# One-hot products in 32 bits, the weight's two parts side by side, four tokens at a time, multiplied on GpSimd

## The chip, the core and the metric

The kernel runs on one core of a Trainium2 chip. The core has TensorE (PE in the rows; PEld is its weight load), VectorE (DVE), ScalarE (ACT), GpSimd (POOL) and SyncE (SP, which issues most of the DMAs). The metric is the device time of one launch in microseconds (us). Before the change it is 2845.25 us, the median of three runs (2843.61 to 2845.64).

## The reference

One transformer layer for 256 prompt tokens and 64 sample tokens of 2048 features: differential attention, a gated chunk MLP, attention to a memory, a gated sum, an output projection, and then a PEER layer, a mixture of 16384 single-row experts. The last layer is where the change is:

```python
def _peer_block(xb, w_query, sub_keys, expert_u, expert_v):
    q = (xb @ w_query).reshape(tb, PEER_HEADS, 2, PEER_HALF)
    s = jnp.einsum('thpc,hpkc->thpk', q, sub_keys).astype(jnp.float32)
    s1, i1 = lax.top_k(s[:, :, 0], PEER_TOPK)
    s2, i2 = lax.top_k(s[:, :, 1], PEER_TOPK)
    ...
    eidx = jnp.take_along_axis(cand_i, top_j, axis=-1)
    g = jax.nn.softmax(top_s, axis=-1).astype(xb.dtype)
    a = jax.nn.gelu(jnp.einsum('td,thkd->thk', xb, expert_u[eidx]), approximate=False)
    return jnp.einsum('thk,thkd->td', g * a, expert_v[eidx])
```

Each token has 8 heads times 16 chosen experts, 128 pairs of an expert and a weight g. An expert's number is 128 * i0 + i1, with i0 and i1 from 0 to 127.

## The kernel before, in words

All instructions are recorded by one Python program that keeps a clock for each engine from assumed costs (the class `Plan`, and `pe_cost`, `dve_cost`, `pool_cost`). Work is cut into tasks (generators); a task goes on when the plan's TensorE clock has passed the assumed end of what it waits for. So the costs and these due times set in which order each engine gets its instructions, and each engine then runs its own list strictly in that order.

TensorE works through a stream of weight pieces. Each half of a piece is loaded by SP into a ring `raw`, ScalarE copies it to `hi` (a 32-bit form with a shorter mantissa, fp32r), VectorE makes `lo` = raw - hi, and TensorE multiplies with hi and lo (class `Stream`, line 413). A ring of four halves of hi and lo lies between VectorE and TensorE. In the PEER layer two phases follow each other. In the first, 128 pieces called Up (16 blocks of three 128x256 products each) compute gelu(x . u) for 256 of the tokens and all 16384 experts; the result goes to `hs`, and for 28 of 32 groups to DRAM. In the second, 128 pieces called Down multiply the weighted hs with expert_v.

The other 64 tokens don't use these dense products. For them GpSimd gathers rows of expert_u and then expert_v (128 indirect DMAs of 1 MB each, tiles `r` and `gs`, queues POOL), and VectorE makes a dot product or a weighted sum from each one (2048 elements a partition: `dots` and `x2s`). These gathers run through both phases.

The dense path needs, for each token t, the 128 x 128 table G_t[i0, i1] of weights, zero where no expert was chosen. It is built by TensorE as a product of one-hot matrices: over the token's 128 choices, one-hot(i0) transposed times (one-hot(i1) * g). That is the task `g_unit` (line 1447), 32 times for 8 tokens each, started by `weights_lane` (line 1339) when Up piece 36 + 74 * t0 / 256 is done, so spread over Up pieces 36 to 110. A unit before the change: VectorE compares `io` (0 to 127) with i0 and i1 (tile `oa`, two operations), multiplies the second with the three bf16 parts of g (tile `ob`, three operations; all 128x1024 in bf16), TensorE makes 3 products of 128x128 for each token (lines 1461 and, through `mm`, 271), added up in PSUM banks `bk`, ScalarE copies each bank of four tokens to `st`, and each 16 tokens SP writes `st` to DRAM (`gd`). When all of them are there, the tables are read back for the Down phase (`gg`).

The task `decode` (line 1365) makes the columns i0, i1 and the parts of g with the token along the free dimension. Line 271 in a row is the helper that records every instruction of VectorE, ScalarE and GpSimd and some of TensorE; tiles tell them apart.

## Time and profile before

| | before |
|---|---|
| median of three runs | 2845.25 us |
| the profiled execution | 2845.33 us, of which the span from first to last instruction 2843.6 us |
| busy: PE, DVE, ACT, POOL | 2788.7, 1870.9, 1101.7, 472.7 us |
| mean granted TensorE clock | 0.963 of 2.4 GHz |
| moved by DMA | 634.75 MB, 223 GB/s over the span |

A group row reads: line, engine, operation, output tile <- input tiles, shapes, count, then busy time in us (overlaps counted once), mean duration in ns, and idle time of the engine just before these instructions with what ended it. Matmuls are pipelined: a duration of 300 ns is longer than the distance to the next start, so rates are read from starts or from counts over a stretch.

### The profile page before, as it was taken

The numbers are of one execution on the slowest core, as the hardware profiler recorded it, in microseconds if no ns is written. First come the engines' busy times: TensorE is split into PE (matmuls) and PEld (weight loads), VectorE is DVE, ScalarE is ACT, GpSimd is POOL, SyncE is SP. The second block draws the span as 40 slices with busy tenths as digits, with TensorE's granted clock in tenths as the row PEclk, the third lists the DMA queues.
The fourth block names the chain that finished last, engine by engine and source line by source line (L and its number), as shares of the span: only waits on it lengthen the run. The fifth ranks groups of instructions, "written<-read, shape, count | busy, mean of one in ns | idle before, by whom it ended". The sixth has DMA issues, their size and how long they took to land.

```text
span 2843.6 us, 42779 instructions
## 1 busy us (share of the span) xinstructions
PE 2788.7 (98%) x17350; PEld 2556.7 (90%) x17350; DVE 1870.9 (66%) x2673; ACT 1101.7 (39%) x1449; POOL 472.7 (17%) x459
## 2 busy tenths in 40 slices
PE   7899999999999999999999999999999899999999
PEld 5899899999999999999899989898997787888887
DVE  8446665444445578898655655555678887888884
ACT  4343444333333343454333333333443334344443
POOL 6423431000001231111100010000112120211100
PEclk9899999999999999999888988888999999999999
DMA  7534343444444544668676666676889888899984
GB/s 220 157 116 126 120 129 124 149 149 151 151 151 156 172 153 163 199 224 283 245 260 234 244 246 230 238 243 229 319 296 330 319 321 294 326 366 341 329 288 140
DMA packets 231909, 634.75 MB, mean 223 GB/s; under 512 B 15776, under 2 KB 70048, under 8 KB 213152
## 3 DMA queue, kind: packets, MB, share of 16 engines
q1 hardware_dynamic: 206624, 474.58, 49.9%
q0 software_dynamic: 21056, 142.76, 13.4%
q10 hardware_dynamic: 4032, 14.68, 1.3%
q8 instruction: 136, 2.23, 0.3%
q14 instruction: 61, 0.50, 0.0%
HBM read 594.08 MB, written 37.88 MB: 222 GB/s over the span
## 4 chain that ended last, share of the span: by engine, by line
PE 85%; DVE 3%; DMA 2%; ACT 1%; issue 1%; ACTq 0%; DVEq 0%
PE mm L413 75%; PE bk L271 5%; PE bk L1461 4%; DMA raw<-pv 2%; DVE lo L271 1%; ACT hi L271 1%; DVE x2s L271 1%; DVE xb L271 0%; ACT xb L271 0%; DVE hs L271 0%; DVE x2t L271 0%; DVE e L271 0%; DVE w L271 0%; ACT w L271 0%; DVE vt L271 0%
## 5 line engine op out<-in xcount | busy, mean ns | idle before, releaser
L271 DVE TENSOR_TENSOR lo<-raw,hi 128x1024 fp32r<-128x1024 f32 (+1 forms) x622 | 874.2, 1408 | 815.2 <-ACT hi L271 814.7
L271 ACT ACTIVATE hi<-raw 128x1024 fp32r<-128x1024 f32 (+1 forms) x622 | 731.5, 1177 | 1052.8 <-PE mm L413 841.4
L413 PE MATMUL mm<-xb,hi 128*128 128x256 f32 x4096 | 802.9, 298 | 0.0
L413 PEld LDWEIGHTS mm<-xb,hi 128*128 128x128 f32 x4096 | 686.1, 205 | 6.3
L413 PE MATMUL mm<-x_g,hi 128*128 128x320 f32 x2688 | 605.1, 314 | 0.0
L413 PE MATMUL mm<-xb,lo 128*128 128x256 f32 x2048 | 601.9, 294 | 0.0
L413 PEld LDWEIGHTS mm<-x_g,hi 128*128 128x128 f32 x2688 | 448.8, 189 | 8.3 <-issue 4.1
L413 PEld LDWEIGHTS mm<-xb,lo 128*128 128x128 f32 x2048 | 417.6, 204 | 0.0
L413 PE MATMUL mm<-x_g,lo 128*128 128x320 f32 x1344 | 416.7, 310 | 0.0
L413 PEld LDWEIGHTS mm<-x_g,lo 128*128 128x128 f32 x1344 | 253.7, 189 | 0.0
L413 PE MATMUL mm<-hi,xb 128*128 128x512 f32 x688 | 217.9, 391 | 0.0
L413 PE MATMUL mm<-hi,w 128*128 128x512 f32 x688 | 217.0, 390 | 0.0
L271 POOL DMA_INDIRECT r<-pur,idx x62 | 81.9, 1321 | 681.0 <-DVE r L271 668.0
L1461 PE MATMUL bk<-ob,oa 128*128 128x128 bf16 x512 | 166.9, 416 | 0.0
L413 PEld LDWEIGHTS mm<-hi,xb 128*128 128x128 f32 x688 | 130.0, 189 | 27.0
L413 PEld LDWEIGHTS mm<-hi,w 128*128 128x128 f32 x688 | 129.2, 188 | 27.2 <-issue 0.5
L271 DVE SCALAR_TENSOR_TENSOR r<-r,xs 128x2048 f32<-128x2048 f32 x62 | 141.6, 2284 | 0.0
L413 PE MATMUL mm<-lo,w 128*128 128x512 f32 x344 | 134.3, 390 | 6.0 <-DVE lo L271 6.0
L413 PE MATMUL mm<-lo,xb 128*128 128x512 f32 x344 | 134.8, 392 | 2.7 <-DVE lo L271 2.7
L271 POOL DMA_INDIRECT r<-pvr,idx x44 | 70.6, 1604 | 387.7 <-DVE x2s L271 386.3
L413 PE MATMUL mm<-xb 128*128 128x512 f32 x504 | 122.4, 398 | 9.0 <-ACT xb L271 5.6
L413 PEld LDWEIGHTS mm<-xb 128*128 128x128 f32 x504 | 96.7, 193 | 30.8 <-ACT xb L271 6.5
(272 smaller groups left out, 3602.3 us busy)
## 6 DMA issues: line engine op xcount, KB each, us to landing
raw<-pu SPq DMA_DIRECT2D x256, 512.0 KB, 4.2
raw<-pv SPq DMA_DIRECT2D x128, 1024.0 KB, 7.2
raw<-win SPq DMA_DIRECT2D x168, 512.0 KB, 3.5
raw<-wbr SPq DMA_DIRECT2D x32, 512.0 KB, 3.5
raw<-wout SPq DMA_DIRECT2D x32, 512.0 KB, 3.5
raw<-wq SPq DMA_DIRECT2D x32, 512.0 KB, 3.6
gd<-st SPq DMA_DIRECT2D x16, 1024.0 KB, 6.8
gg<-gd SPq DMA_DIRECT2D x16, 1024.0 KB, 12.6
```

The costliest lines, as they stand in the source:

```text
L271: r = f(*a, **k)
L413: nc.tensor.matmul(o, stays, moves, start=first, stop=last and n == len(products) - 1)
L1461: nc.tensor.matmul(o, oa[:, 0, :, k], ob[:, j, :, k], start=j == 0, stop=False)
```

## The change

A unit now holds 4 tokens, and 64 units are spread over Up pieces 36 to 112. VectorE compares in 32 bits (two operations of 128x512, one for i1 into `ob`, one for i0 into `oa`). GpSimd multiplies the one-hot of i1 with the high part of g (`wH`) and with the rest (`wL`, kept in a part of `cst` that is no longer needed), so that both lie side by side in `ob` (two operations of 128x512). TensorE makes one product of 128x256 in fp32r for each token; the two halves of its output are the tables of the high and of the low part. ScalarE copies the high half of two tokens to `st` (128x256, twice), VectorE adds the low half from PSUM (128x256, twice). The one-hot tiles get three buffers instead of two, a unit takes two PSUM banks, the bf16 tiles and the cost rules for bf16 are gone.

```diff
-TU = 8
-GE0, GEN = 36, 110
+GE0, GEN = 36, 112
...
-        R["io"] = q.tile([128, 128, TU], BF16, name="io")
-        pool.tensor_copy(R["io"], cst[:, C_IO:C_IO + 128, None].to_broadcast([128, 128, TU]))
-        OA = Slots(plan, q, "oa", [128, 2, 128, TU], BF16, 2)
-        OB = Slots(plan, q, "ob", [128, 3, 128, TU], BF16, 2)
+        OA = Slots(plan, q, "oa", [128, 4, 128], F32R, 3)
+        OB = Slots(plan, q, "ob", [128, 4, 2, 128], F32R, 3)
...
-        for t0 in range(0, DN, TU):
+        for t0 in range(0, DN, 4):
             yield from need(("up", GE0 + (GEN - GE0) * t0 // DN))
...
-        col = lambda nm: R[nm][:, None, t0:t0 + TU].to_broadcast([128, 128, TU])
-        dve.tensor_tensor(oa[:, 0], R["io"], col("k0"), op=ALU.is_equal)
-        dve.tensor_tensor(oa[:, 1], R["io"], col("k1"), op=ALU.is_equal)
-        yield
-        for j in range(3):
-            dve.tensor_tensor(ob[:, j], oa[:, 1], col(f"w{j}"), op=ALU.mult)
-            yield
-        for a in range(TU // 4):
-            bk, = yield from take(BK)
-            for k in range(4 * a, 4 * a + 4):
-                o = bk[:, 128 * (k % 4):128 * (k % 4) + 128]
-                for j in range(2):
-                    nc.tensor.matmul(o, oa[:, 0, :, k], ob[:, j, :, k], start=j == 0, stop=False)
-                    plan.clk["pe"] += 0.067
-                mm(o, oa[:, 0, :, k], ob[:, 2, :, k], start=False, stop=True)
-            yield
-            o = t0 % TB + 4 * a
-            act.activation(st[:, :, o:o + 4], bk.rearrange("p (t i) -> p i t", t=4), AF.Copy)
-            BK.give(bk)
+        io = cst[:, None, C_IO:C_IO + 128].to_broadcast([128, 4, 128])
+        col = lambda nm: R[nm][:, t0:t0 + 4, None].to_broadcast([128, 4, 128])
+        dve.tensor_tensor(ob[:, :, 1, :], io, col("iT1"), op=ALU.is_equal)
+        pool.tensor_tensor(ob[:, :, 0, :], ob[:, :, 1, :], col("wH"), op=ALU.mult)
+        pool.tensor_tensor(ob[:, :, 1, :], ob[:, :, 1, :], col("wL"), op=ALU.mult)
+        dve.tensor_tensor(oa, io, col("iT0"), op=ALU.is_equal)
+        yield
+        b2 = yield from take(BK, BK)
+        for k in range(4):
+            mm(b2[k // 2][:, (k % 2) * 256:(k % 2) * 256 + 256], oa[:, k, :], ob[:, k].rearrange("p j i -> p (j i)"),
+               start=True, stop=True)
         OA.give(oa)
         OB.give(ob)
+        yield
+        o, work = t0 % TB, []
+        for a, bk in enumerate(b2):
+            v = bk.rearrange("p (t j i) -> p t j i", t=2, j=2)
+            s2 = st[:, :, o + 2 * a:o + 2 * a + 2].rearrange("p i t -> p t i")
+            act.activation(s2, v[:, :, 0], AF.Copy)
+            work.append((s2, v[:, :, 1], bk))
+        yield
+        for s2, x, bk in work:
+            dve.tensor_tensor(s2, s2, x, op=ALU.add)
+            BK.give(bk)
```

How the engines' lists change is shown at one place, about Up piece 60 to 63; a number behind a tile's name only counts tiles, so equal numbers are one tile, and the helper's line is 271 before and 269 now. VectorE before, where `lo` is the stream's second part, `dots` a sample token's dot product, and `oa` and `ob` belong to one unit of 8 tokens:

```order
L271 TENSOR_TENSOR oa_14339<-io,r_80 128x1024 x2
L271 TENSOR_TENSOR lo<-raw,hi 128x1024
L271 TENSOR_TENSOR ob_14340<-oa_14339,r_80 128x1024
L271 TENSOR_TENSOR lo<-raw,hi 128x1024
L271 TENSOR_TENSOR ob_14340<-oa_14339,r_80 128x1024
L271 TENSOR_TENSOR lo<-raw,hi 128x1024
L271 SCALAR_TENSOR_TENSOR r_80,dots<-r_80,xs 128x2048
L271 TENSOR_TENSOR ob_14340<-oa_14339,w_8746 128x1024
```

VectorE now, from the comparisons of one unit (`ob_14287`) to the additions into `st_14285` that belong to it:

```order
L269 TENSOR_TENSOR ob_14287<-cst,r_80 128x4x128
L269 TENSOR_TENSOR oa_14286<-cst,r_80 128x512
L269 TENSOR_TENSOR st_14000<-st_14000,bk_14295 128x2x128
L269 TENSOR_TENSOR st_14000<-st_14000,bk_14296 128x2x128
L269 TENSOR_TENSOR lo<-raw,hi 128x1024 x2
L269 TENSOR_TENSOR ob_14362<-cst,r_80 128x4x128
L269 TENSOR_TENSOR oa_14361<-cst,r_80 128x512
L269 SCALAR_TENSOR_TENSOR r_80,dots<-r_80,xs 128x2048
L269 TENSOR_TENSOR lo<-raw,hi 128x1024
L269 TENSOR_TENSOR st_14285<-st_14285,bk_14405 128x2x128
L269 TENSOR_TENSOR st_14285<-st_14285,bk_14406 128x2x128
```

The five operations of a unit have become four, for half as many tokens, and the last two stand behind the comparisons of the next unit.

GpSimd at the same place now, with what each waits for (before, its list held nothing but the gathers here):

```order
L269 TENSOR_TENSOR ob_14287<-ob_14287,wH 128x4x128 [waits DVE_49,PE_49]
L269 TENSOR_TENSOR ob_14287<-ob_14287,cst 128x4x128 [waits Pool_49]
L269 DMA r_80<-pur,idx 128x2048 [waits DMASW1_49]
L269 TENSOR_TENSOR ob_14362<-ob_14362,wH 128x4x128 [waits DVE_49,PE_49]
L269 TENSOR_TENSOR ob_14362<-ob_14362,cst 128x4x128 [waits Pool_49]
```

The gathers now stand between the pairs of multiplications.

TensorE now, one unit's four products between two blocks of Up pieces (before, 24 products and 24 weight loads in two bursts for 8 tokens stood there):

```order
L409 MATMUL mm_14355<-xb,lo 128x256
L269 MATMUL bk_14405<-ob_14287,oa_14286 128x256 x2
L269 MATMUL bk_14406<-ob_14287,oa_14286 128x256 x2
L409 MATMUL mm_14355<-xb,hi 128x256 x2
L409 MATMUL mm_14355<-xb,lo 128x256
```

Counted over Up pieces 36 to 112, the lists hold: TensorE 3648 products of the stream in both, and of one-hot products 768 before and 252 now (4 more right behind); VectorE 152 `lo` in both, 51 dots before and 44 now, 160 one-hot operations before, and 128 comparisons and 126 additions now; GpSimd 51 gathers before, 44 gathers and 128 multiplications now. In the last 16 halves of the Down phase's 128, the lists hold no gather before and 6 now; the four products that fold the sample tokens' sums (`bk<-x2s`) stand 9 halves from the end before and 5 from the end now.

## Rows read from the trace of the kernel before

**Rows 1.** The page: each engine's busy time, share of the span and instructions; then the chain that ended last, by engine and by line.

```profile
PE 2788.7 (98%) x17350; PEld 2556.7 (90%) x17350; DVE 1870.9 (66%) x2673; ACT 1101.7 (39%) x1449; POOL 472.7 (17%) x459
...
PE 85%; DVE 3%; DMA 2%; ACT 1%; issue 1%; ACTq 0%; DVEq 0%
PE mm L413 75%; PE bk L271 5%; PE bk L1461 4%; DMA raw<-pv 2%; DVE lo L271 1%; ACT hi L271 1%; DVE x2s L271 1%; DVE xb L271 0%; ACT xb L271 0%; DVE hs L271 0%; DVE x2t L271 0%; DVE e L271 0%; DVE w L271 0%; ACT w L271 0%; DVE vt L271 0%
```

**Rows 2.** Stretches: the start and end, the length, then busy us and instructions of PE, PEld, DVE, ACT and POOL, the granted clock, the DMA share and GB/s. The first runs from the start of Up piece 36 to that of piece 112, the second holds pieces 112 to 119, the third the rest of the program from the end of the last Up.

```profile
1346.34:2015.32 668.98, 668.98 (x4418) 605.43 (x4417) 392.12 (x414) 220.05 (x292) 66.25 (x53) 0.87 0.69 242
2015.32:2061.40 46.08, 46.08 (x386) 46.08 (x385) 33.48 (x35) 20.50 (x28) 6.71 (x4) 1.00 0.93 342
...
2107.64:2843.60 735.96, 712.78 (x3113) 583.62 (x3111) 587.39 (x556) 293.73 (x260) 98.17 (x58) 0.99 0.84 305
```

**Rows 3.** TensorE's timeline through one unit: start us, length us, engine, line, operation, tiles, shape, how many in a row.

```profile
1365.42 0.66 PE L1461 MATMUL bk<-ob,oa 128*128 128x128 bf16 x2
1365.91 0.41 PE L271 MATMUL bk<-ob,oa 128*128 128x128 bf16 x1
1366.14 0.65 PE L1461 MATMUL bk<-ob,oa 128*128 128x128 bf16 x2
...
1371.85 0.41 PE L413 MATMUL mm<-xb,lo 128*128 128x256 f32 x1
...
1372.48 0.41 PE L413 MATMUL mm<-xb,lo 128*128 128x256 f32 x1
...
1376.46 0.40 PE L413 MATMUL mm<-xb,hi 128*128 128x256 f32 x2
```

**Rows 4.** Groups of the same stretch as the first of rows 2, shapes kept apart.

```profile
L271 DVE TENSOR_TENSOR lo<-raw,hi 128x1024 fp32r<-128x1024 f32 x152 | 185.9, 1224 | 276.4 <-ACT hi L271 276.4
...
L271 ACT ACTIVATE hi<-raw 128x1024 fp32r<-128x1024 f32 x152 | 161.0, 1060 | 283.1 <-PE mm L413 281.3 <-DVE oa L271 1.8
L271 DVE SCALAR_TENSOR_TENSOR r<-r,xs 128x2048 f32<-128x2048 f32 x51 | 116.5, 2284 | 0.0
...
L271 POOL DMA_INDIRECT r<-pur,idx x52 | 66.2, 1273 | 600.3 <-DVE r L271 588.3 <-issue 12.0
L271 DVE TENSOR_TENSOR ob<-oa,r 128x1024 bf16<-128x1024 bf16 x64 | 43.8, 685 | 0.0
L271 DVE TENSOR_TENSOR oa<-io,r 128x1024 bf16<-128x1024 bf16 x64 | 41.2, 684 | 0.0
...
L271 ACT ACTIVATE hs<-mm 128x256 f32<-128x256 f32 x76 | 27.9, 367 | 0.0
L271 DVE TENSOR_TENSOR ob<-oa,w 128x1024 bf16<-128x1024 bf16 x32 | 21.9, 684 | 0.0
L271 DVE DVE_READ_ACCUMULATOR r<-r,xs 128x1 f32 x51 | 4.2, 82 | 0.0
```

**Rows 5.** Groups of the whole span that are nearest to VectorE's new operations: an addition-like one of 256 elements, a comparison of 1024 elements, and one that reads PSUM.

```profile
L271 DVE TENSOR_TENSOR hs<-hs,gg 128x256 f32<-128x256 f32 x128 | 51.7, 418 | 0.0
...
L271 DVE TENSOR_TENSOR r<-mm,rb_x 128x320 f32<-128x320 f32 x56 | 27.0, 483 | 0.0
...
L271 DVE TENSOR_TENSOR big<-xt,cst 128x1024 f32<-128x1024 f32 x12 | 14.8, 1232 | 0.0
```

**Rows 6.** Timelines early in the program, where GpSimd multiplies beside VectorE: first VectorE and GpSimd between 12.6 and 21 us, then two `lo` at 1312 us, where GpSimd only issues a gather, then the slowest `lo` that met one GpSimd multiplication (of 640 elements).

```profile
14.19 6.27 DVE L271 TENSOR_TENSOR lo<-raw,hi 128x1024 fp32r<-128x1024 f32 x3
...
12.64 1.35 POOL L271 TENSOR_TENSOR r<-r,sq 128x512 f32<-128x512 f32 x1
13.95 1.22 POOL L271 TENSOR_TENSOR sq<-r 128x512 f32<-128x512 f32 x1
15.24 2.16 POOL L271 TENSOR_TENSOR r<-r,sq 128x512 f32<-128x512 f32 x1
17.36 2.02 POOL L271 TENSOR_TENSOR sq<-r 128x512 f32<-128x512 f32 x1
...
1312.20 2.35 DVE L271 TENSOR_TENSOR lo<-raw,hi 128x1024 fp32r<-128x1024 f32 x2
...
59.15 2.56 DVE L271 TENSOR_TENSOR lo<-raw,hi 128x1024 fp32r<-128x1024 f32 x1
```

**Rows 7.** Timelines of GpSimd and VectorE about 126 us: four GpSimd multiplications in a row, and beside them a VectorE operation that reads PSUM (`r<-mm,rb_x`) and one that reads SBUF alone (`lo`).

```profile
126.03 7.93 POOL L271 TENSOR_TENSOR r<-r 128x512 f32<-128x512 f32 x4
...
126.96 0.48 DVE L271 TENSOR_TENSOR r<-mm,rb_x 128x320 f32<-128x320 f32 x1
128.93 1.60 DVE L271 TENSOR_TENSOR lo<-raw,hi 128x1024 fp32r<-128x1024 f32 x1 [1.49 <-ACT hi L271]
```

**Rows 8.** More stretches, columns as in rows 2: where VectorE is busiest with TensorE never idle, one where TensorE waits, and the last two before the end.

```profile
1207.00:1278.00 71.00, 71.00 (x598) 71.00 (x598) 66.80 (x110) 38.88 (x54) 7.84 (x10) 1.00 0.65 219
...
2201.00:2272.00 71.00, 63.30 (x268) 50.93 (x267) 56.69 (x61) 26.91 (x27) 8.25 (x6) 0.95 0.89 322
...
2698.00:2769.00 71.00, 71.00 (x315) 58.80 (x314) 62.04 (x60) 29.55 (x26) 4.02 (x4) 1.00 0.84 302
2769.00:2840.00 71.00, 69.89 (x315) 55.91 (x313) 33.01 (x29) 25.45 (x24) 0.00 (x0) 1.00 0.40 135
```

**Rows 9.** DMA issues: tiles, queue, kind, count, KB each where it is known, median us from issue to landing.

```profile
r<-pvr,idx POOLq DMA_INDIRECT x44, 8.6
```

More of the change, by code (lines that the diff above doesn't have):

```diff
@@ L14 @@
 U32 = mybir.dt.uint32
-BF16 = mybir.dt.bfloat16
 AF = mybir.ActivationFunctionType
@@ L292, in pe_cost @@
     n = size(a[2]) / (2.4e3 if op == "matmul" and a[2].dtype == F32R else 0.6e3)
-    if op == "matmul" and a[2].dtype == BF16:
-        return 0.0133 + size(a[2]) / 2.4e3
     return max(0.107, n + 0.0133) if op == "matmul" else 0.216
@@ L305, in dve_cost @@
         size(k["in_values"]) if op in ("max_index", "match_replace") else size(out)
-    return 0.16 + n / 0.96e3 * (6.2 if op == "reciprocal" else 0.5 if out.dtype == BF16 else 1)
+    return 0.16 + n / 0.96e3 * (6.2 if op == "reciprocal" else 1)
 def pool_cost(op, a, k):
@@ L1189, in open_route @@
         p = open_pool(route, "route")
-        for n, nm in enumerate(("k0", "k1", "w0", "w1")):
-            R[nm] = r1[:, KT * T + 128 * n:KT * T + 128 * n + 128].bitcast(BF16)
-        R["w2"] = p.tile([128, DN], BF16, name="w2")
-        R["wr"] = p.tile([128, 128], F32, name="wr")
+        for n, nm in enumerate(("iT0", "iT1")):
+            R[nm] = r1[:, KT * T + DN * n:KT * T + DN * n + DN]
+        R["wH"] = p.tile([128, DN], F32R, name="wH")
+        R["wL"] = cst[:, C_COS:C_COS + DN]
         for n in ("idx", "wS", "dots", "act"):
@@ L1354, in weights_lane @@
             spawn(g_unit(t0, oa, ob, OA, OB, ST, st))
-        while len(gdone) < DN // TU:
+        while len(gdone) < DN // 4:
             yield
@@ L1410, in decode @@
             c = slice(i * 128, i * 128 + n)
-            wT = bk[:, 256:256 + n]
-            for a, nm in enumerate(("k0", "k1", "w0")):
+            for a, nm in enumerate(("iT0", "iT1", "wH")):
                 act.activation(R[nm][:, c], bk[:, a * 128:a * 128 + n], AF.Copy)
-            wr = R["wr"][:, :n]
-            dve.tensor_tensor(wr, wT, R["w0"][:, c], op=ALU.subtract)
-            yield
-            act.activation(R["w1"][:, c], wr, AF.Copy)
-            dve.tensor_tensor(R["w2"][:, c], wr, R["w1"][:, c], op=ALU.subtract)
+            dve.tensor_tensor(R["wL"][:, c], bk[:, 256:256 + n], R["wH"][:, c], op=ALU.subtract)
             BK.give(bk)
@@ L1762, in hybrid_kernel @@
         sync.dma_start(outs["dbg2"], xb[:, 1].bitcast(F32))
-        for n, nm in enumerate(()):
+        for n, nm in enumerate(("iT0", "iT1", "wH")):
             sync.dma_start(outs["dbg3"][:, n], R[nm].bitcast(F32))
```

## The prediction

> **What bounds the kernel now.** I read the page first: TensorE is busy for 98% of the span and carries 85% of the chain that ended last, VectorE 3% [rows 1]. So time is won or lost where TensorE's list gets shorter, or where it begins to wait. Then the stretches, to see what the stage of the one-hot products costs. From the start of Up piece 36 to that of piece 112 pass 668.98 us, TensorE never idle, its granted clock 0.87, VectorE 392 us busy. The eight pieces behind it, without one-hot products, take 46.08 us at a clock of 1.00 [rows 2]: 5.76 us a piece, 0.120 us for each of the 48 products in one. 76 pieces at that rate are 437.8 us, so the one-hot products cost 231.2 us on the path. The timeline shows both parts of that. Three bf16 products start 0.72 us after the three before (1365.42, 1366.14), about 0.233 us each: 768 of them are 179 us. And behind a unit's two bursts the stream runs at half speed, three products in 0.63 us (1371.85 to 1372.48) where three take 0.36 at the full clock, until 1376.46 [rows 3]: the granted clock has fallen to 1.2 GHz after the bursts, and is back at 2.4 GHz after a stretch of dense stream. That is the other 52 us.
>
> The groups of the stage show who has room. VectorE idles 276 us before `lo`, waiting for `hi`, which ScalarE makes when TensorE frees a place; GpSimd issues 52 gathers and otherwise waits [rows 4]. So TensorE alone is the bound there.
>
> **The change, part by part.** TensorE loses 768 bf16 products and gets 256 of 128x256 in fp32r, of the same form as the stream's, so 0.120 us each: 30.7 us. The bursts are four products long instead of twelve, and none is slow, so I expect no fall of the clock from them. TensorE's own need for the stage is then 437.8 + 30.7 = 468.5 us, 200.5 us less. That is the end of the sum if nothing else becomes late.
>
> VectorE is what may become late. Its list in the stage, by count and duration: 152 `lo` at 1.224 us = 186.0; 44 dots at 2.284 + 0.082 = 104.1 [rows 4]; 128 comparisons of 512 elements, not in the trace, bounded by 418 ns for 256 elements and 1232 for 1024 [rows 5], on the line between them 0.69 us = 88.3; 126 additions of 256 elements with one input in PSUM, between 0.37 us (ScalarE's row of that size) and the 0.483 us of 320 elements [rows 4, 5], I take 0.42 = 52.9. Sum 431 us. Durations overlap at their ends: before, the groups sum to 416 us (186.0 + 116.5 + 4.2 + 160 x 0.684) where VectorE is busy for 392 [rows 2, 4], a factor of 0.94. So VectorE needs about 406 us by itself, less than TensorE.
>
> But 128 GpSimd multiplications now run beside it. Alone, one of two inputs and 512 elements takes 1.35 us. Beside VectorE it takes 2.16, and the three `lo` next to such multiplications take 6.27 us where two without them take 2.35 [rows 6]: 2.09 instead of 1.175 each, 0.915 us more for each multiplication met. They run in turn, hardly at the same time. Where VectorE reads PSUM it isn't slowed: 0.48 us beside GpSimd's 7.93 us, the same as its mean of 0.483 [rows 5, 7]. The comparisons, `lo` and dots all read two tensors in SBUF, the additions don't. So each multiplication costs VectorE from nothing (it falls beside an addition, or a wait) to 1.34 us (2.56 against 1.22, the slowest `lo` of rows 6); I take 0.915, the mean of the densest rows: 128 x 0.915 = 117 us, and 406 + 117 = 523 us. Now VectorE has more to do than TensorE. It can't be busy all the time, since its list is strictly in order; the highest share that the trace shows is 66.80 of 71 us, 94% [rows 8]. 523 / 0.94 = 556 us. The bounds by the same working: with no collision 406 / 0.94 = 432, under TensorE's 468.5, which then stands; with 1.34 us for each one (406 + 172) / 0.94 = 615.
>
> [...]
>
> ScalarE gets 128 copies of 256 elements at about the 0.367 us of its `hs` row, 47 us, for 64 larger ones, and is busy for 220 of 669 us: nothing [rows 2, 4]. GpSimd has 128 x 1.35 to 2.16 = 173 to 276 us of multiplications and 44 gather issues of 1.27 us [rows 4, 6]: under 340 of 556 us, no bound, but gathers queue behind multiplications that wait for comparisons, and the dots, and VectorE's list behind them, wait for gathers. The 6% of idle time above holds this. The clock: TensorE will wait some 90 us in short pieces; where it waits now, busy for 63.30 of 71 us, the clock is 0.95 [rows 8]. It would have to fall to 468.5 / 556 = 0.84 before TensorE is the bound again, so I cost it at nothing; that cover goes if VectorE's need is smaller than I think.
>
> What stands later: 7 gathers less lie in the stage, and 6 of them now in the last 16 halves of Down, whose stretches have none to four today and a DMA share of 0.84 and 0.40 [rows 8]. Their 1 MB each at 302 GB/s is 3.5 us, 21 us in all if nothing hid them; the room in the last stretch alone is 43 us, so I take 3 us. The fold of the sample tokens' sums moves to 5 halves before the end, about 5 x 5.7 = 29 us, which still covers a late gather (8.6 us to landing [rows 9] and one 2.35 us sum). The rest of the Down phase, 735.96 us, has the same counts [rows 2].
>
> **Sum.** Against the profiled execution, 2845.3 us (span 2843.6 and 1.7 around it; the median of the runs shown is 2845.25, the same): 2845.3 - (669.0 - 556) + 3 = 2735 us.
>
> **Rivals.**
> *TensorE stays the bound.* If the multiplications meet VectorE seldom, or its list absorbs them, the stage takes 468.5 us: 2845.3 - 200.5 + 3 = 2648 us. For it: VectorE's 406 us leave 62 us free, and 94% busy beside a TensorE that never idled did occur [rows 8]. Against it: every `lo` beside a GpSimd multiplication in rows 6 and 7 is longer than those without one. [...]
>
> *The unit's own chain decides.* A place freed by TensorE is followed by `hi` 1.06, `lo` 1.22 + 0.92, two comparisons 1.38, a multiplication 1.35, often a dot 2.28 that goes first, the second multiplication 1.35, then the product: 9.56 us [rows 4 to 6], where TensorE has 1.19 pieces and four products, 7.3 us, in between. Were it so for every unit, the stage would take 64 x 9.56 = 612 us: 2845.3 - 57 + 3 = 2791 us. For it: GpSimd's list has both multiplications in a row and the second waits for the first. Against: three buffers of `ob`, and two units are under way at once in VectorE's list.
>
> *Slower than before.* VectorE's additions stand in its list behind the next unit's comparisons and wait for ScalarE's copies, which wait for the products. If the product is late, VectorE, by then the bound, stands still before the addition, and with it the next `lo` and comparisons. One such stand costs four products 0.48, a `hi` in front of the copies 1.06 and two copies 0.73: 2.27 us [rows 4]. In all 64 units that is 145 us on top of 556: 2845.3 + 32 + 3 = 2880 us. It decides from (669 - 556) / 64 = 1.8 us a unit on. Against: in the order shown, three `lo`, a dot and two comparisons, over 7 us, lie between a unit's comparisons and its additions.
>
> That the change doesn't spread the units isn't likely: the counted lists hold 12 to 14 copies in every eight pieces.
>
> **How the numbers follow.** VectorE and GpSimd in turn, 2735 us (2690 to 2780): 0.57. TensorE the bound, 2648 (2635 to 2690): 0.18. The chain, 2791 (2780 to 2835): 0.18. Slower, 2880: 0.07, of which a part ends just at no change. The range of 2655 to 2810 leaves out half of the slower part of the chain, the last case, and the fastest end: about 0.2. A measurement of this kernel can tell 0.2% (6 us) from no change. Faster 0.92, within that 0.02, slower 0.06.
>
> **What would show it.** Right: in the stage, `lo` and the comparisons average 0.3 us and more above their time alone, the multiplications about 2 us instead of 1.35, the additions stay near 0.42; VectorE is busy for over 90% of some 556 us; TensorE waits for `lo` or `ob` by some 90 us in all; one-hot products start 0.12 us apart; the granted clock stays above 0.9. Wrong: a stage near 470 us with TensorE never idle (the first rival); VectorE idle before the additions or before `ob` for over 60 us (the other two); a clock under 0.84; a Down phase over 20 us longer.

## The result, and the profile after

The changed kernel takes 2718.55 us, the median of four runs (2710.47 to 2721.75), beside 2845.44 us for the kernel before on the same chip (2843.61 to 2845.84): a ratio of 0.9551, 95% interval 0.9529 to 0.9572. The profiled execution took 2721.75 us. The page says where the engines stand; against [rows 1] GpSimd is 287 us busier, VectorE 91, and TensorE 175 less.

```profile
PE 2614.0 (96%) x16838; PEld 2436.5 (90%) x16838; DVE 1961.5 (72%) x2767; ACT 1130.3 (42%) x1511; POOL 760.2 (28%) x586
```

The stretches answer to [rows 2]: the stage from Up piece 36 to 112, the eight pieces behind it, the rest after the last Up, and then two stretches of four Up pieces each within the stage, one with a long wait and one without.

```profile
1346.50:1890.12 543.62, 492.34 (x3902) 483.01 (x3901) 467.45 (x494) 248.33 (x354) 338.79 (x173) 0.97 0.79 282
1890.12:1936.68 46.56, 46.56 (x390) 46.56 (x389) 34.75 (x38) 21.61 (x30) 9.80 (x7) 1.00 0.97 351
...
1982.93:2720.00 737.07, 712.56 (x3112) 583.42 (x3111) 600.15 (x567) 293.60 (x261) 114.78 (x66) 0.99 0.86 312
...
1454.92:1488.44 33.52, 27.89 (x211) 27.69 (x209) 25.00 (x30) 13.80 (x20) 17.08 (x10) 0.90 0.72 254
1749.48:1775.42 25.94, 25.13 (x206) 24.63 (x205) 23.74 (x29) 12.79 (x18) 14.02 (x9) 1.00 0.87 317
```

The whole gain is in the stage: 668.98 to 543.62 us. The Down phase took 735.96 and takes 737.07. But within the stage the second and third columns tell two things that were not forecast: TensorE is not busy for 51.28 us, and VectorE, which was to be the bound, is busy for only 467 of 544 us, 86%.

The groups of the stage, against [rows 4]:

```profile
L269 DVE TENSOR_TENSOR lo<-raw,hi 128x1024 fp32r<-128x1024 f32 x152 | 208.7, 1384 | 73.0 <-ACT hi L269 72.6
...
L269 POOL TENSOR_TENSOR ob<-ob,cst 128x512 fp32r<-128x512 f32 x64 | 167.4, 2616 | 5.0
...
L269 DVE SCALAR_TENSOR_TENSOR r<-r,xs 128x2048 f32<-128x2048 f32 x44 | 120.7, 2744 | 0.0
...
L269 POOL TENSOR_TENSOR ob<-ob,wH 128x512 fp32r<-128x512 f32 x64 | 86.5, 1351 | 181.5 <-DVE ob L269 131.3 <-PE mm L409 49.9
L269 POOL DMA_INDIRECT r<-pur,idx x45 | 86.2, 1917 | 28.1 <-DVE r L269 21.9 <-issue 3.0 <-DVE st L269 0.6
L269 DVE TENSOR_TENSOR st<-st,bk 128x256 f32<-128x256 f32 x126 | 72.3, 618 | 3.2 <-ACT st L269 3.2
...
L269 ACT ACTIVATE st<-bk 128x256 f32<-128x256 f32 x126 | 68.8, 652 | 69.1 <-PE bk L269 68.3 <-ACT hs L269 0.5
...
L269 DVE TENSOR_TENSOR ob<-cst,r 128x512 fp32r<-128x512 f32 x64 | 47.1, 736 | 0.0
...
L269 DVE TENSOR_TENSOR oa<-cst,r 128x512 fp32r<-128x512 f32 x64 | 43.7, 683 | 0.0
```

`lo` and the dots are longer than before, by 0.16 and 0.46 us on average, so VectorE is slowed where GpSimd multiplies. But the one who pays most is GpSimd: its second multiplication takes 2.62 us on average, the first 1.35, where one that meets nothing takes 1.04 (all 63 in the run below that has one on each engine). The waits of the stage say who waits for that:

```profile
ACT hi L269 <- PE mm L409: 225.7, 143, 4.9
...
POOL ob L269 <- DVE ob L269: 131.3, 34, 9.2
...
DVE lo L269 <- ACT hi L269: 72.6, 58, 5.0
...
PE bk L269 <- POOL ob L269: 51.1, 39, 5.7
```

All of TensorE's idle time is the last row: 39 of 64 units wait for GpSimd. A wait is a little longer than it shows, because it is counted from the end of the product before, whose row is 0.28 us long where the next start should follow after 0.12:

```profile
1735.52 0.28 PE L409 MATMUL mm<-xb,lo 128*128 128x256 f32 x1
1736.63 0.74 PE L269 MATMUL bk<-ob,oa 128*128 128x256 f32 x4 [0.83 <-POOL ob L269]
```

From 1735.52 to 1736.63 pass 1.11 us, 0.99 more than 0.12, and 0.83 of them count as idle. Added up from the starts, some 8 us of the stage are such time, counted as busy.

The longest waits look like this on the timelines of GpSimd, VectorE and TensorE (start, length):

```profile
1462.05 6.67 POOL L269 TENSOR_TENSOR ob<-ob,cst 128x512 fp32r<-128x512 f32 x1
...
1638.78 6.70 POOL L269 TENSOR_TENSOR ob<-ob,cst 128x512 fp32r<-128x512 f32 x1
...
1462.07 2.35 DVE L269 TENSOR_TENSOR lo<-raw,hi 128x1024 fp32r<-128x1024 f32 x2
1464.33 0.69 DVE L269 TENSOR_TENSOR ob<-cst,r 128x512 fp32r<-128x512 f32 x1
1464.94 0.69 DVE L269 TENSOR_TENSOR oa<-cst,r 128x512 fp32r<-128x512 f32 x1
1465.54 2.28 DVE L269 SCALAR_TENSOR_TENSOR r<-r,xs 128x2048 f32<-128x2048 f32 x1
1467.75 0.08 DVE L269 DVE_READ_ACCUMULATOR r<-r,xs 128x1 f32 x1
...
1615.89 4.02 DVE L269 TENSOR_TENSOR lo<-raw,hi 128x1024 fp32r<-128x1024 f32 x2
...
1468.77 1.22 PE L269 MATMUL bk<-ob,oa 128*128 128x256 f32 x4 [5.63 <-POOL ob L269]
...
1469.79 0.63 PE L409 MATMUL mm<-xb,hi 128*128 128x256 f32 x2
1470.22 0.41 PE L409 MATMUL mm<-xb,lo 128*128 128x256 f32 x1
1470.43 0.63 PE L409 MATMUL mm<-xb,hi 128*128 128x256 f32 x2
```

VectorE ran five operations with two SBUF inputs at their own speed (two `lo` in 2.35 us, as in [rows 6] without GpSimd), and GpSimd's multiplication, begun 0.02 us before, stood for all of them. It ended at 1468.72, 0.97 us after the dot's read of its accumulator began, and about that, 1.04 us, is what it takes where it meets nothing. The row at 1638.78 is a second such case. TensorE waited 5.63 us, and then the stream ran at half speed: three products in 0.64 us (1469.79 to 1470.43), the granted clock 0.50 from 1468.77 to 1474.70 and 0.90 over the four Up pieces around it. At 1615.89 two `lo` took 4.02 us: there GpSimd got its turn in between, with multiplications of 1.05 us (from 1615.79) and 1.91 us (from 1616.92). Both happen. By the starts in the timelines, all nine multiplications of over 3 us in this stage, and all five gathers of over 4 us, began within 0.12 us of the start of a `lo`, right behind a unit's two additions, which end at about the same time as its first multiplication. That isn't the whole rule: the multiplication at 1797.55 began so too and had its turn after one `lo`, in 2.11 us (that `lo` took 1.21 us, the next 2.06).

### The profile page after: what moved, and what is told of

The parts are those of the page before. It is cut to its first block, busy times and chain, and to the rows that moved or that the text cites. A ratio compares the mean times of both kernels' runs of the same rounds, so it can differ in the third digit from the quotient of the medians.

```text
span 2720.0 us, 42175 instructions
## 1 busy us (share of the span) xinstructions
PE 2614.0 (96%) x16838; PEld 2436.5 (90%) x16838; DVE 1961.5 (72%) x2767; ACT 1130.3 (42%) x1511; POOL 760.2 (28%) x586
## 5 line engine op out<-in xcount | busy, mean ns | idle before, releaser
L269 DVE TENSOR_TENSOR lo<-raw,hi 128x1024 fp32r<-128x1024 f32 (+1 forms) x622 | 897.0, 1447 | 607.4 <-ACT hi L269 606.6
L409 PE MATMUL mm<-xb,hi 128*128 128x256 f32 x4096 | 752.5, 286 | 0.0
L409 PEld LDWEIGHTS mm<-xb,hi 128*128 128x128 f32 x4096 | 647.2, 194 | 0.0
L409 PE MATMUL mm<-xb,lo 128*128 128x256 f32 x2048 | 583.9, 285 | 0.0
L409 PEld LDWEIGHTS mm<-xb,lo 128*128 128x128 f32 x2048 | 397.9, 194 | 0.0
L269 POOL TENSOR_TENSOR ob<-ob,cst 128x512 fp32r<-128x512 f32 x64 | 167.4, 2616 | 5.0
L269 DVE SCALAR_TENSOR_TENSOR r<-r,xs 128x2048 f32<-128x2048 f32 x60 | 157.3, 2622 | 0.0
L269 POOL TENSOR_TENSOR r<-r 128x320 f32<-128x320 f32 (+2 forms) x39 | 39.5, 1015 | 402.1 <-DVE r L269 397.1
L269 POOL DMA_INDIRECT r<-pur,idx x60 | 108.1, 1802 | 122.5 <-DVE r L269 115.3
L269 POOL TENSOR_TENSOR ob<-ob,wH 128x512 fp32r<-128x512 f32 x64 | 86.5, 1351 | 181.5 <-DVE ob L269 131.3
```

The costliest lines, as they stand in the source:

```text
L269: r = f(*a, **k)
L409: nc.tensor.matmul(o, stays, moves, start=first, stop=last and n == len(products) - 1)
```

## The experiments

The sum that has to be explained is 543.6 us of stage against 468.5 that TensorE needs by the prediction: 51.3 us of waits, and 23.8 us by which TensorE's busy 492.3 exceed its need. Of the 23.8, some 16 are half speed (171 products that hold the engine for 0.22 us on average instead of 0.12), and the other 8 the part of the waits that counts as busy. Two readings were open: VectorE, slowed by collisions, sets the stage (as forecast), or the product comes late and the rest follows from that.

**A lag of 4 us in the plan before the products.**

```diff
         dve.tensor_tensor(oa, io, col("iT0"), op=ALU.is_equal)
         yield
+        plan.task.at += 4.0
         b2 = yield from take(BK, BK)
```

> The same work, but a unit's four products are placed at least 4 us later in TensorE's list (and what follows from them too). Theory L (late products): in the changed kernel TensorE waits 51 us in front of the one-hot products for GpSimd's second multiplication and loses about 24 us more to the clock that falls after such waits, so with 4 us more the waits fall under 15 us, the clock in the stage rises to 0.99, the stage from Up 36 to 112 takes 485 to 500 us instead of 544, and the whole 2665 to 2680 us. Theory V (my forecast: VectorE's list, stretched by collisions with GpSimd, is the bound): the stage stays within 8 us of 544 and the whole at 2710 to 2725 us, since VectorE has the same work.

Measured 2720.75 us, ratio 0.9554 (0.9534 to 0.9573), the same as the change. The waits became fewer and longer, 12 with 39.8 us instead of 39 with 51.1:

```profile
PE bk L269 <- POOL ob L269: 39.8, 12, 5.8
```

The stage, and the eight pieces behind it, took:

```profile
1346.51:1874.00 527.49, 487.74 (x3899) 485.30 (x3898) 464.56 (x489) 245.21 (x352) 352.59 (x170) 0.96 0.79 284
1874.00:1926.63 52.63, 48.69 (x395) 48.49 (x394) 38.56 (x42) 22.78 (x32) 16.82 (x9) 0.97 0.97 350
```

So the stage lost 16 us, but 6 of them are found again in the eight pieces behind it (46.56 in the change), where one more unit's products now stand, and the rest after the last Up took 750.6 us instead of 737.1. The stage fits neither expectation; the whole time lies where the forecast's theory had it. The waits behind a starved multiplication (up to 7.79 us here) stayed. Why the Down phase grew was not followed up; these are single profiled executions, and the four runs spread over 14 us.

**The multiplications on VectorE, in the same order.**

```diff
+    alt = Engine(plan, "pool", nc.vector, pool_cost)
...
-        pool.tensor_tensor(ob[:, :, 0, :], ob[:, :, 1, :], col("wH"), op=ALU.mult)
-        pool.tensor_tensor(ob[:, :, 1, :], ob[:, :, 1, :], col("wL"), op=ALU.mult)
+        alt.tensor_tensor(ob[:, :, 0, :], ob[:, :, 1, :], col("wH"), op=ALU.mult)
+        alt.tensor_tensor(ob[:, :, 1, :], ob[:, :, 1, :], col("wL"), op=ALU.mult)
```

> The two multiplications of a unit are issued to VectorE at the same places of the order; GpSimd only issues gathers. VectorE gets 128 x about 0.63 us = 81 us more and loses the collisions (about 24 us on lo, 20 on dots, 3 on comparisons), so it is busy for about 500 us. Theory L: no product waits for a turn at SBUF, TensorE's waits for ob fall under 20 us, the stage takes 505 to 520 us (VectorE nearly full), the whole 2680 to 2700. Theory V gives about the same, 515 us. If the order of the lists alone makes the products late, whatever engine multiplies, the waits for ob stay near 50 us and the stage at 540 or more.

Measured 2684.47 us, 0.9437 (0.9421 to 0.9453), 34 us faster than the change although VectorE got 126 operations more. The plan goes on counting them on GpSimd's clock. Both theories had expected about this, so the time alone doesn't tell them apart. The stretch of the stage:

```profile
1347.39:1852.37 504.98, 477.06 (x3903) 470.14 (x3902) 497.56 (x616) 248.00 (x354) 58.65 (x45) 1.00 0.84 300
```

`lo` is back at 1.219 us, a multiplication takes 0.692, and VectorE is busy for 98.5% of the stage. Here VectorE is the bound; in the changed kernel, at 86%, it is not.

**No multiplication** (left out: the weights, both halves of the product take the bare one-hot).

```diff
-        pool.tensor_tensor(ob[:, :, 0, :], ob[:, :, 1, :], col("wH"), op=ALU.mult)
-        pool.tensor_tensor(ob[:, :, 1, :], ob[:, :, 1, :], col("wL"), op=ALU.mult)
...
-            mm(b2[k // 2][...], oa[:, k, :], ob[:, k].rearrange("p j i -> p (j i)"),
+            mm(b2[k // 2][...], oa[:, k, :], ob[:, k, 1:2, :].to_broadcast([128, 2, 128]),
```

> Leaves out the two multiplications by the weight (the products take the bare one-hot matrix for both halves): what the multiplications cost in all. Both theories: TensorE's own 468.5 us is the bound, stage 470 to 485 us, the whole 2645 to 2662, the clock 0.99 or more, no waits for ob. If the stage stays over 500 us, something else than GpSimd holds it: the additions or VectorE's comparisons.

Measured 2651.64 us, 0.9322 (0.9307 to 0.9338).

```profile
1346.37:1814.85 468.48, 468.48 (x3906) 468.48 (x3905) 418.14 (x494) 245.42 (x354) 63.39 (x45) 1.00 0.89 326
```

This is TensorE's need of the prediction, 437.8 + 30.7 = 468.5, to the tenth: never idle, clock 1.00. The 75 us by which the changed kernel's stage is longer all hang on the multiplications. VectorE needs 418.1 us without them (406 forecast).

**The multiplications done, but unread** (left out: the weights; GpSimd writes to a tile `ox` that nothing reads, the products take the bare one-hot).

```diff
+        R["ox"] = q.tile([128, 4, 2, 128], F32R, name="ox")
...
+        pool.tensor_tensor(R["ox"][:, :, 0, :], ob[:, :, 1, :], col("wH"), op=ALU.mult)
+        pool.tensor_tensor(R["ox"][:, :, 1, :], ob[:, :, 1, :], col("wL"), op=ALU.mult)
...
```

> Leaves the weights out of the products, but GpSimd does its 128 multiplications all the same, into a tile that nobody reads: the collisions with VectorE without TensorE's wait for their result. Theory V (collisions make VectorE's list the bound): stage 520 us or more, as in the changed kernel, with VectorE busy for over 90%. Theory L (the wait for a late product costs the 75 us above TensorE's own 468.5): stage 468 to 480 us, no waits for ob, the clock at 0.99 or more, the whole 2645 to 2665 us, though the multiplications still take about 2 us each.

Measured 2668.37 us, 0.9371 (0.9355 to 0.9387). The stretch of the stage:

```profile
1346.67:1833.41 486.74, 474.85 (x3903) 470.67 (x3901) 479.44 (x489) 247.32 (x354) 320.04 (x171) 1.00 0.86 310
```

This splits the 75 us, in the order in which the two are taken away. With the collisions and no product waiting for a multiplication, the stage is 486.7: 18.3 us stay with the collisions, which make VectorE the bound (479.4 busy, 98.5%), and 56.9 us go with the wait for the late product. The split is not exact for the changed kernel, since the collisions fall otherwise here. A multiplication cost VectorE (479.4 - 418.1) / 126 = 0.49 us here; in the changed kernel it is (467.5 - 418.1) / 128 = 0.39. The stage lies between the two expectations, much nearer to that of the late product, though outside both.

**The two halves added in PSUM**, two 128x128 products for each token and no additions on VectorE.

```diff
+            for j in range(2):
+                mm(bk[:, k * 128:k * 128 + 128], oa[:, k, :], ob[:, k, j], start=j == 0, stop=j == 1)
...
-            dve.tensor_tensor(s2, s2, x, op=ALU.add)
```

> The high and low products are added up in PSUM (two products of 128x128 for each token instead of one of 128x256), so VectorE's 128 additions go (78 us by their 618 ns) and ScalarE copies once for four tokens. Theory V: VectorE's need falls by over 70 us, TensorE's own need is the bound again, stage 475 to 495 us. Theory L: the additions are the only VectorE operations beside which GpSimd gets at SBUF without waiting; without them its multiplications come later, TensorE's waits for ob stay at 50 us or grow, stage 530 to 570 us.

Measured 2726.65 us, 0.958 (0.9564 to 0.9596). VectorE lost 126 additions and the stage hardly moved, 540.8 us, which speaks again against VectorE's length as the bound. But the case is mixed: TensorE was busy for 507.8 us, 70 over the stream's 437.8. Where nothing waits, the eight products of a unit start 0.11 us apart:

```profile
1375.05 1.01 PE L269 MATMUL bk<-ob,oa 128*128 128x128 f32 x8
1375.89 0.45 PE L409 MATMUL mm<-xb,hi 128*128 128x256 f32 x2
```

512 of them at 0.11 are 56 us, instead of 31 for the 256 long ones; the other 14 are mostly half speed and the hidden part of the waits, as above. TensorE's waits for `ob` fell from 51 to 33 us, where the theory of the late product had expected them to stay or grow. The second multiplication took 2.97 us at most, with no PSUM-reading additions at all:

```profile
L269 POOL TENSOR_TENSOR ob<-ob,cst x64: 1039/1904/2969, 1356.0 to 1882.6; 128x512 fp32r<-128x512 f32 x64
```

These are minimum, median and maximum in ns; for the changed kernel the same view of the tile has:

```profile
L269 POOL TENSOR_TENSOR ob<-ob,cst x64: 1040/2112/6704, 1356.8 to 1888.5; 128x512 fp32r<-128x512 f32 x64
```

So the idea that GpSimd gets its turn mainly beside those additions does not hold. Rather the reverse: without them no gather and no multiplication took over 3 us, and only 10 of 181 began within 0.12 us of the start of a VectorE operation with two SBUF inputs (37 of 172 in the changed kernel).

**The multiplications elsewhere**, in three ways, to be rid of the collisions; the plan still counts them on GpSimd's clock. First eight ScalarE copies with a scale for each unit:

```diff
+    alt = Engine(plan, "pool", nc.scalar, lambda *_: 0.37)
...
+        for j, nm in enumerate(("wH", "wL")):
+            for k in range(4):
+                alt.activation(ob[:, k, j, :], ob[:, k, 1, :], AF.Copy, scale=R[nm][:, t0 + k:t0 + k + 1].bitcast(F32))
```

> ScalarE makes the two weighted one-hot matrices (8 copies of 128 elements with the weight as scale, instead of GpSimd's two multiplications). 512 copies at 0.2 to 0.28 us put 100 to 140 us on a ScalarE busy for 248 of 544 us. Theory L: no turn at SBUF is fought over, so TensorE's waits for ob fall under 15 us and the stage to 470 to 495 us, the whole 2648 to 2675. If the order of the lists makes products late whatever engine multiplies, or hi comes late behind the copies in ScalarE's list, the stage stays above 515 us.

Measured 2732.59 us, 0.9603 (0.9587 to 0.9619). A copy took 0.39 us instead of the 0.2 to 0.28 assumed, eight of them 3.1 us, and TensorE waited 37.6 us in the stage of 545.2. Second, comparing and multiplying in one VectorE operation for each token and half:

```diff
+    alt = Engine(plan, "pool", nc.vector, lambda *_: 0.37)
...
+        for k in range(4):
+            t = t0 + k
+            for j, nm in enumerate(("wH", "wL")):
+                alt.tensor_scalar(ob[:, k, j, :], cst[:, C_IO:C_IO + 128], R["iT1"][:, t:t + 1], R[nm][:, t:t + 1].bitcast(F32),
+                                  op0=ALU.is_equal, op1=ALU.mult)
```

> VectorE compares and multiplies in one operation with two scalars for each token and part (8 of 128 elements a unit), no GpSimd multiplication and no comparison for i1. 512 operations at 0.2 to 0.28 us are 102 to 143 us, where the run with the multiplications on VectorE has 128 x 0.69 + 64 x 0.69 = 132 us by durations. VectorE is then busy for 470 to 510 us and is the bound or next to it: stage 475 to 515, the whole 2655 to 2695 us, TensorE's clock at 1.00.

Measured 2748.86 us, 0.9663 (0.9647 to 0.9679). 512 operations of 0.35 us, not the 0.2 to 0.28 assumed, stood in for 64 comparisons on VectorE and the 128 multiplications, VectorE was busy for 518.5 of the stage's 575.7 us, and TensorE waited 86.1. Third, the high part on VectorE (`alt`) and the low part on ScalarE (`scl`):

```diff
+    alt = Engine(plan, "pool", nc.vector, pool_cost)
+    scl = Engine(plan, "pool", nc.scalar, lambda *_: 0.37)
...
+        alt.tensor_tensor(ob[:, :, 0, :], ob[:, :, 1, :], col("wH"), op=ALU.mult)
+        for k in range(4):
+            scl.activation(ob[:, k, 1, :], ob[:, k, 1, :], AF.Copy, scale=R["wL"][:, t0 + k:t0 + k + 1].bitcast(F32))
```

> The multiplication by the high part goes to VectorE, the one by the low part to ScalarE as four copies with a scale; GpSimd keeps its gathers alone. Theory T (the stage is the floor 468.5 us plus what TensorE waits for the late product, and the floor shows as soon as no engine is over some 90% busy and nothing is starved): VectorE 418 us (the run without multiplications) + 64 x 0.69 = 462 us, ScalarE 375.7 - 256 x 0.387 + ... = 326 us or so, stage 475 to 500 us, TensorE's waits below 20 us, whole kernel 2655 to 2685 us. Rival S (what is late is the chain one-hot, product, matmul in itself, whichever engine multiplies; ScalarE's copies stand behind its stage evictions in order): stage over 520 us, TensorE's waits over 30 us on ScalarE's tile, whole kernel over 2700 us.

Measured 2715.34 us, 0.9542 (0.9526 to 0.9558), stage 534.8, as its rival said.

```profile
DVE lo L269 <- ACT hi L269: 47.4, 41, 2.6
...
PE bk L269 <- ACT ob L269: 34.7, 31, 2.1
DVE st L269 <- ACT st L269: 21.1, 17, 1.3
```

ScalarE's copies stand in its list for VectorE (`ob`), so `hi` and `st` behind them come late for VectorE. With 462.6 us busy and 68.5 us of such waits VectorE fills 531 of the 534.8 us. All three have no collision and still a late product: a multiplication behind in-order lists is late for more reasons than the starved one. How much of this lateness is the plan's, which charged these operations to the wrong engine's clock, was not tried; the last two experiments show that a price or a lag can remove such waits.

**One multiplication on each.** The high part stays on GpSimd, the low part goes to VectorE.

```diff
+    alt = Engine(plan, "pool", nc.vector, pool_cost)
...
         pool.tensor_tensor(ob[:, :, 0, :], ob[:, :, 1, :], col("wH"), op=ALU.mult)
-        pool.tensor_tensor(ob[:, :, 1, :], ob[:, :, 1, :], col("wL"), op=ALU.mult)
+        alt.tensor_tensor(ob[:, :, 1, :], ob[:, :, 1, :], col("wL"), op=ALU.mult)
```

> The multiplication by the high part stays on GpSimd, the one by the low part goes to VectorE. Theory T (waits come from the second multiplication of GpSimd, which stands up to 6.7 us while VectorE runs back to back): with one multiplication on GpSimd it can still be starved, so waits stay but are fewer: VectorE about 467 + 64 x 0.69 - 9 (half the collisions) = 500 us, stage 500 to 525 us, single waits up to 6 us, whole kernel 2680 to 2705 us. Rival C (the collisions alone cost the time and halve): VectorE 485 us, stage 485 to 495 us, waits below 15 us, whole kernel 2660 to 2675 us.

Measured 2714.73 us, 0.954 (0.9524 to 0.9556); both expectations missed. The stage took 534.9 us for a reason that neither had:

```profile
DVE ob L269 <- POOL ob L269: 78.4, 63, 1.2
```

The low part is made in place, so VectorE's multiplication must wait until GpSimd has read the one-hot, 1.24 us in each of 63 units. VectorE's 453.9 us busy and these 78.4 are 532 of 534.9 us. There was no collision left (`lo` 1.222 us), because VectorE stood still meanwhile.

**The layout alone.** The kernel before with its three bf16 products, but the tiles laid out as in the change, the token outside and the 128 one-hot elements side by side. Before, neighbouring elements of a product's operand lay 8 elements of 2 bytes apart.

```diff
-        OA = Slots(plan, q, "oa", [128, 2, 128, TU], BF16, 2)
-        OB = Slots(plan, q, "ob", [128, 3, 128, TU], BF16, 2)
+        OA = Slots(plan, q, "oa", [128, 2, TU, 128], BF16, 2)
+        OB = Slots(plan, q, "ob", [128, 3, TU, 128], BF16, 2)
...
-                    nc.tensor.matmul(o, oa[:, 0, :, k], ob[:, j, :, k], start=j == 0, stop=False)
+                    nc.tensor.matmul(o, oa[:, 0, k], ob[:, j, k], start=j == 0, stop=False)
```

> The kernel before, with the token outside and the 128 indices inside in its bf16 tiles, so that TensorE reads the one-hot tiles without steps. If the steps of 16 bytes made its bf16 products start 0.233 us apart, they now start 0.06 to 0.12 us apart, the bursts are short and the clock stays near 1.00: TensorE needs 485 to 530 us for its stage. VectorE's 160 operations may take 1.2 us instead of 0.684, since the scalar column is then the repeated operand along the inside. Stage 495 to 545 us instead of 669, the whole 2670 to 2720. If instead bf16 products as such are slow here, they stay at 0.233 us and the whole at 2835 to 2855.

One run took 2679.19 us, less than the changed kernel. The 768 products cost 490.1 - 437.8 = 52 us, where they cost 231.2 before.

```profile
1345.32:1849.61 504.29, 490.07 (x4418) 484.20 (x4417) 471.03 (x414) 219.53 (x292) 83.28 (x53) 1.00 0.88 318
```

VectorE pays for it: its bf16 operations take 1.219 us where they took 0.684 [rows 4], and 14.2 us of TensorE's waits are left. A product took 0.233 us before, with steps of 16 bytes, and takes about 0.07 now, with the elements side by side; why the step costs that is not shown. Both operands of a product were changed at once; which of them made it slow was not tried.

**The layout with the planner told so.** The plan's price of a bf16 operation on VectorE is set to what was measured.

```diff
-    return 0.16 + n / 0.96e3 * (6.2 if op == "reciprocal" else 0.5 if out.dtype == BF16 else 1)
+    return 0.16 + n / 0.96e3 * (6.2 if op == "reciprocal" else 0.92 if out.dtype == BF16 else 1)
```

> The kernel before with its bf16 one-hot tiles laid out with the token outside, and the planner's price of a bf16 operation on VectorE set to what it measured there (1.22 us for 128x1024 instead of 0.69). Theory B (in the kernel before, the stride of the products' operands is what the change gets rid of, not the third product): TensorE's need is 490 us, and with right prices its 14 us of waits fall below 8: stage 490 to 500 us, whole kernel 2662 to 2678 us, faster than the changed kernel by 40 to 55 us. Rival: VectorE at 471 of 504 us already holds the stage, and the prices only move the waits: stage 500 to 512 us, whole kernel 2676 to 2690 us.

Measured 2656.12 us (2655.76 to 2657.28), 0.9335 (0.932 to 0.9351): the fastest kernel here that computes all, 62 us below the change, and faster than the expectation (stage 490 to 500 us, whole 2662 to 2678). The stretch of the stage:

```profile
1345.44:1830.13 484.69, 484.69 (x4418) 481.92 (x4417) 462.12 (x406) 219.69 (x292) 79.71 (x49) 1.00 0.88 320
```

TensorE never waits, its granted clock is 1.00, and VectorE keeps up at 95%. The products start three in 0.17 us, 0.057 each, where [rows 3] had 0.233:

```profile
1511.49 0.28 PE L1461 MATMUL bk<-ob,oa 128*128 128x128 bf16 x2
1511.60 0.22 PE L271 MATMUL bk<-ob,oa 128*128 128x128 bf16 x1
1511.66 0.27 PE L1461 MATMUL bk<-ob,oa 128*128 128x128 bf16 x2
```

**The layout with the old price and a lag of 3 us.**

```diff
+        plan.task.at += 3.0
+        yield
         for a in range(TU // 4):
```

> As the run with the token outside, prices left, and the 12 products of a unit due 3 us later in the plan. Theory B (TensorE's 14 us of waits there are single late one-hots, and a lag covers them): waits below 4 us, stage 490 to 496 us, whole kernel 2663 to 2672 us. Rival (as the 4 us lag did in the changed kernel: a lag makes the waits fewer and longer and moves time behind the stage): stage 495 to 505 us, the rest after the last Up longer by 5 us or more, whole kernel 2675 to 2690 us.

Measured 2660.32 us, 0.9352 (0.9336 to 0.9367), stage 486.1 (4 us below the expectation), TensorE's waits 1.1 us:

```profile
1345.73:1831.87 486.14, 485.03 (x4418) 482.01 (x4417) 470.68 (x416) 219.44 (x292) 86.87 (x54) 1.00 0.89 330
```

Here a lag does what it failed to do in the changed kernel: the waits for one-hots in the run with the layout alone were 19 of 2.5 us at most, 13.9 us in all, and GpSimd has no multiplication here that could be starved. In the changed kernel itself, another price for GpSimd's multiplications (the plan has 1.48 us for each) was not tried.

## Why the prediction was right in its time, and wrong in a part of its reason

The forecast was 2735 us with 2655 to 2810, the result 2718.55. The stage took 543.6 us instead of 556, and the rest is as forecast. That the number came so near is partly luck: the engine that was to set the stage does not set it. Of the prediction's own signs, the multiplications' mean (1.98 us), the products' distance and the clock above 0.9 came true; VectorE over 90% busy, `lo` and the comparisons 0.3 us longer and additions near 0.42 us did not. Step by step:

- *TensorE's need, 468.5 us.* Right: 468.48 without the multiplications, with products 0.12 us apart and no fall of the clock from their bursts (granted 1.00). The 0.233 us that it gets rid of, though, belong to the old layout and not to three bf16 products as such: side by side they take 0.057.
- *VectorE's own list, 406 us.* 418.1. The additions took 0.618 us and not 0.42, 25 us more, of which a larger overlap of the operations took back half. They ran at the same 0.615 to 0.626 in every kernel that has them, with GpSimd multiplying or not, so what failed is the interpolation from rows of other shapes ([rows 4, 5]), and not a collision. PSUM alone doesn't make it, as 320 elements with one input there took 0.483 [rows 5]; the additions also read and write `st` with a step, which was not tried apart. ScalarE's copies into the same tile took 0.652 us instead of 0.367, which cost nothing.
- *The collision, 0.915 us for each multiplication, charged to VectorE.* This is the step that failed. The two engines do slow each other, but VectorE pays 0.39 us, and the multiplications stand for 0.31 (first) and 1.58 us (second) on average. The 1.35 us that the prediction took for a multiplication alone was none: the row at 12.64 ran beside VectorE operations on `x_m`, and alone it is 1.04. The densest rows before had three `lo`, of 2.06 to 2.31 us each, and GpSimd in strict turns [rows 6]; in the stage VectorE often ran on, and GpSimd stood up to 6.7 us.
- *VectorE the bound at 94% of its time.* Wrong in this kernel: 86% busy, and where VectorE is the bound it reaches 98.5% (the multiplications moved to it). The 556 us came near because two errors met by luck: VectorE's need taken 56 us too high (523 against 467), and a late product that the sum didn't have.
- *The clock costs nothing.* It cost some 16 us, at a mean granted clock of 0.97; the rest of the 23.8 (492.3 - 468.5) is the part of the waits that counts as busy. The condition named, that the cover goes if VectorE's need is smaller, is what came true: with TensorE the engine that everything hangs on, half-speed stretches after a long wait add to the path. The trace gives the clock as a share of full speed, not in GHz: 0.50 behind a unit's bursts before (1371.85 to 1376.33) and 1.00 from 1376.46 on; now 0.50 behind the wait of 5.63 us (1468.77 to 1474.70) and 1.00 again from 1474.89 on.
- *TensorE waits some 90 us, for `lo` or `ob`.* 51.3 us, all for `ob`. The rival of the unit's own chain is what happens, but in 39 of 64 units, and mostly by under a microsecond; five waits (5.63, 2.80, 4.97, 2.58 and 5.67 us), each behind a multiplication that stood for 6.65 to 6.70 us, are 42% of it. VectorE's 72.6 us of idle time before `lo` go with it, since `hi` waits for TensorE to free a place. They fall to 4.2 us in the run with unread multiplications, where VectorE is the bound, and are still 48.9 in the run without any, where TensorE is: they show who has time left, and not a cost.
- *The rival in which TensorE stays the bound at 2648 us.* It is what the multiplications prevent: without them the kernel takes 2651.6.
- *Slower than before.* VectorE stood before its additions for 3.2 us in all; the price of that rival was never paid.
- *The Down phase, 3 us.* 1.1 us longer.

What stays open: by which rule the two engines take turns (once GpSimd waits for five operations, once only for one; in the changed kernel the long stands all begin with a `lo`, but with the multiplications unread, first ones that began some 0.22 us into a comparison took up to 4.84 us as well), and why the lag of 4 us lengthened the Down phase.

## What to carry to other kernels

The layout of a matmul's operands can cost more than the number of products: the three bf16 products for a token cost 231 us of the stage with elements 16 bytes apart and 52 with elements side by side, and the layout with a right price in the planner beats the rewrite (2656 against 2719 us). When work moves to GpSimd beside a VectorE that runs back to back on SBUF, charge the collision to GpSimd's latency too (here 0.31 and 1.58 us, against VectorE's 0.39) and ask who waits for its result; if that is TensorE in order, the clock adds to the wait (some 16 us to 59 here). To part a collision from a late result, do the work and leave its result unread, and look whether the collisions stay as they were.

## What the runs showed of the hardware that was not expected

- GpSimd can be starved for several VectorE instructions, not only for one: 6.70 us for a multiplication that takes 1.04 alone. In the rows from 1462.05 VectorE's next instruction went first five times in a row.
- The issue of a gather can be held as well. It took 1.27 us before [rows 4] and 1.92 on average in the changed kernel; five of its 45 took 4.32 to 6.55 us, and each of these ended 0.85 to 0.86 us after the last of a run of VectorE operations with two SBUF inputs. With the multiplications on VectorE, busy for 98.5%, none took over 1.69 us, so a busy VectorE alone doesn't do it. The longest stood beside two `lo`, two comparisons and a dot:

```profile
1609.22 6.55 POOL L269 DMA_INDIRECT r<-pur,idx  x1
```

- An fp32r product of 128 columns costs nearly as much as one of 256: 0.11 us from start to start against 0.12 (the run with the halves added in PSUM).
- VectorE's bf16 operations lost almost half their speed (0.684 to 1.219 us) in the layout with the token outside, where the token's column is repeated along the innermost dimension; whether this repetition or another stride made it was not tried.
- Small operations are dear for their size: 128 elements take 0.387 us on ScalarE (a copy with a scale from a column) and 0.35 us on VectorE (compare and multiply with two columns), where a VectorE multiplication of 512 elements takes 0.69.
